# Prompt attention with the values two steps behind the scores, opened together with them, and six probability buffers

## The chip, the cores and the metric

The kernel runs on one core of a Trainium2 chip. The core has a matmul engine (PE, with its weight loads shown as PEld), three engines for elementwise work (DVE, ACT, POOL) and SP, whose queue issues most of the DMA transfers. Each engine works through its own instructions in the order in which they were written down when the kernel was built; an instruction that has to wait for a semaphore holds up all that stand behind it on that engine. The metric is the time of one execution on the device in microseconds (us); lower is better.

## The reference

One layer of a decoder for a prompt of 1024 tokens and a batch of 8 x 4 new tokens, in float32. What matters here is the attention of the prompt: 8 heads of 64 in 2 groups of 4 heads that share keys and values, with three branches that are added with a gate each.

```python
def nsa_block(q, gates, q_pos, ctx, kw, vw, w_pos):
    ...
    p_c = masked_softmax(s_c, m_c)                      # compressed blocks of keys
    o_c = jnp.einsum('bqghc,bcgd->bqghd', p_c.astype(vc.dtype), vc)
    ...
    p_s = masked_softmax(s_s, m_s)                      # chosen blocks (for the prompt: all that are valid)
    o_s = jnp.einsum('bqghn,bgqnd->bqghd', p_s.astype(v_sel.dtype), v_sel)
    ...
    p_w = masked_softmax(s_w, m_w)                      # the last 512 keys and the query itself
    o_w = jnp.einsum('bqghw,bwgd->bqghd', p_w.astype(vw.dtype), vw)
    g = jax.nn.sigmoid(gates.astype(jnp.float32)).astype(q.dtype)
    return g[..., 0:1] * o_c + g[..., 1:2] * o_s + g[..., 2:3] * o_w
```

The prompt has 16 blocks of 64 keys and 16 are chosen, so the second branch sees every key up to the query. Before and after the attention stand a combined input projection, a convolution module, gates and two output projections, for prompt and new tokens alike.

## The kernel before

The kernel has four stages. The input projection and the attention of the new tokens (with gathers from the paged caches) fill the first 850 us. The prompt attention follows, woven with the last tiles of the input projection, the norm and the pointwise product of the convolution and the merge of the second branch. At about 1265 us the output products begin (tiles `v`).

The order on each engine is not written by hand. The code yields pieces of several streams in turn (`_mixed`, `late_weave`: so many pieces of the prompt stream for so many of the others), and a scheduler with a timing model of its own then places the instructions on the engines by that order and by when it thinks that inputs and buffers are ready. A change in the prompt stream therefore re-plans all engines from its first step on.

The prompt stream (`prompt_stream`, L1523) runs over the 2 groups `g`, the 8 query tiles `qt` of 128 queries and two pairs of heads `hp`: 32 steps. A step has these parts:

- `queries` (L1295) loads the queries of a tile twice, one below the other, into `ldq`. ACT copies the upper half to `Qst` (rounded for the fast matmul format) and the lower half to `ldh`, and DVE puts the rest of the rounding into the lower half of `Qst`.
- `prompt_scores` (L1413) makes for both heads `e` and both branches `i` (0: all keys, 1: the window) scores in a bank pair `S` (two of them), subtracts the maximum (DVE, L1470), takes the exponential with its sum (ACT, L1426) into a buffer `P`, and scales P by gate over sum: on DVE for branch 0 (L1485), for branch 1 on POOL for one head (L1487) and on ACT for the other (L1489). `P0` and `P1` have four buffers each, two of which one step takes.
- `prompt_values` (L1492) transposes the probabilities in groups of four 128 x 128 blocks into a bank `tr` (PE, L1512; three banks, shared with the woven streams), splits a group into a rounded half `pth` (ACT, L1334) and the rest `ptl` (DVE, L1335), three buffers each, and multiplies both with the values into `acc` (PE, L1502 and L1503), one group behind the transposes.
- `prompt_open` (L1402) does the same for the compressed branch: it transposes `Pc`, splits it, and its two products (L1409, L1410) are the first to write `acc`. There is one bank `acc` (`ps_a`). `put` (L1338) reads it out at the end of a tile: two copies on ACT (L1342, L1343) and two additions on DVE (L1346).
- `prompt_c` (L1367) makes the compressed probabilities `Pc` for both groups while `g` is 0 and stores them in `pc_d`, from where group 1 loads them; `Pc` has two buffers.

Scores of step n are woven with the values of step n-1 (L1536 to L1540). `prompt_open` of a tile is called when its first step's scores are done (L1542).

Woven with this are `branches` (L1549: three loads `obt`, `obl` of the new tokens' branches, two additions on DVE, four small transposes on PE, L1559; the loads use buffers of `pth` and `ptl`), `points` (L1685: loads `x` from `s_d`, ACT's rounding `sh`, POOL's rest `sl`, products with `pwh`, `pwl`), and `late` (L1733: the merge, then `gated` tiles with loads `gat`, and four loads `wa` of w_pa that ACT copies at L1748).

Of the kernel before, what the change touches and what calls it, by code (L numbers as in the profile page):

```python
# [119 lines left out]
def _emit(ctx, tc, I, O, dbg=None, stop=None):  # L120
# [1150 lines left out]
    with ExitStack() as P3:  # L1271
# [23 lines left out]
        def queries(g, qt):  # L1295
            Qst = pq.tile([128, 4, 128], F32R, name="Qst", tag="Qst", bufs=2)
            x = pq.tile([128, 4, 128], F32, name="ldq", tag="ldq", bufs=2)
            src = qT_d[g * 256:(g + 1) * 256, qt * 128:(qt + 1) * 128].rearrange("(h d) q -> d h q", h=4)
            sp.dma_start(x[:64], src)
            sp.dma_start(x[64:], src)  # L1300
            hi = pq.tile([128, 4, 128], F32R, name="ldh", tag="ldh", bufs=1)
            for o, r, on in ((Qst, slice(0, 64), QC & 1), (hi, slice(64, 128), QC >> 1)):
                if on:
                    pool.tensor_copy(o[r], x[r])
                else:
                    act.activation(o[r], x[r], AF.Copy)
            dve.tensor_tensor(Qst[64:], x[64:], hi.bitcast(F32)[64:], op=ALU.subtract)
            return Qst
# [93 lines left out]
        def prompt_open(g, qt, Pc):  # L1402
# [10 lines left out]
        def prompt_scores(g, qt, hp, Qst, S):  # L1413
# [10 lines left out]
            def exps(e, i, sv, W, n):  # L1424
                P = pP.tile([128, 1024 if i == 0 else 640], F32, name="P", tag=f"P{i}", bufs=4)
                act.activation(P[:, :W].rearrange("p (c w) -> p c w", c=n), sv, AF.Exp,  # L1426
                               bias=nm[:, e, i:i + 1], accum_out=l[:, e, i:i + 1])
                Ps.append(P)
# [63 lines left out]
        def prompt_values(g, qt, hp):  # L1492
            Ps, Vs, lo_k = PU.pop((g, qt, hp))
            acc = PU[g, qt]
# [28 lines left out]
        def prompt_stream():  # L1523
            prev = None
            Q = queries(0, 0)
            for g in range(2):
                S = stacks(g)
                for qt in range(8):
# [3 lines left out]
                    else:  # L1532
                        P = pq.tile([128, 8, 64], F32, name="Pc", tag="Pc", bufs=2)
                        sp.dma_start(P.rearrange("p a c -> p (a c)"), pc_d[qt * 128:(qt + 1) * 128, :])
                    for hp in range(2):
                        streams = [(prompt_scores(g, qt, hp, Q, S), 2 if qt < 4 else 4)]  # L1536
                        if prev:
                            n = min(prev[1], 4) + prev[1] + 2
                            streams.append((prompt_values(*prev), (n + 1) // 2))
                        yield from _mixed(*streams)  # L1540
                        if hp == 0:
                            prompt_open(g, qt, P)  # L1542
                        elif (g, qt) != (1, 7):
                            Q = queries(*divmod(g * 8 + qt + 1, 8))
                        prev = (g, qt, hp)
            yield from prompt_values(*prev)
# [330 lines left out]
```

## Time and profile before

| what | value |
|---|---|
| three runs, median (lowest to highest) | 1423.98 us (1417.65 to 1424.43) |
| the profiled execution | 1420.95 us |
| its span, first to last instruction | 1419.2 us |
| mean granted clock of PE in it | 0.979 of 2.4 GHz |
| prompt attention in the span | about 848 to 1265 us |
| busy share of PE, DVE, ACT, POOL over the span | 94%, 76%, 51%, 46% |

PE is busy nearly all the time, but a matmul's end is modelled, so busy does not mean at its peak; what can be read well is where PE stands idle and who ended it. A granted clock of 1.00 is 2.4 GHz, 0.50 is 1.2 GHz, and values between them are means over a stretch.

### The profile page before, as it was taken

The page shows a single profiled execution, that of the slowest core. Times are in us where ns is not written, and L with a number is a line of the kernel's source. Part 1 is how long each engine was busy: PE and PEld are TensorE (multiplying, and loading weights), DVE is VectorE, ACT ScalarE, POOL GpSimd, SP SyncE. Part 2 cuts the span into 40 slices and gives each one's busy share as a digit, 9 for nine tenths or more (in the row PEclk, how much of TensorE's full clock was granted, in tenths as well). Part 3 has the DMA queues.
Part 4 walks back from the last instruction along what each step waited for, and adds up shares of the span by engine and source line. Part 5 has one row for each costly group of instructions (what it writes and reads, how often), then busy time and mean ns, then how long its engine had stood idle before and what let it go on. Part 6 is the DMA issues. An engine that isn't in the chain of part 4 may idle for free.

```text
span 1419.2 us, 25556 instructions
## 1 busy us (share of the span) xinstructions
PE 1337.1 (94%) x9689; PEld 1202.6 (85%) x9689; DVE 1078.7 (76%) x1915; ACT 720.5 (51%) x1323; POOL 646.0 (46%) x537
## 2 busy tenths in 40 slices
PE   5999989879999999999999999999889999899997
PEld 4998989879899999788877898889778899789876
DVE  7888886878887848887956945978777988888233
ACT  5454445545443634554554335766666876653311
POOL 2388884886884605554454202434564221321200
PEclk9999999989999999999999999999979999999999
DMA  7666566566665418797788565543553633416421
GB/s 256 189 193 215 179 183 209 188 212 197 196 203 195 153 52 298 236 356 265 262 301 287 173 165 163 154 121 98 177 152 98 192 118 102 133 51 196 182 92 46
DMA packets 184358, 256.87 MB, mean 181 GB/s; under 512 B 27348, under 2 KB 137508, under 8 KB 183971
## 3 DMA queue, kind: packets, MB, share of 16 engines
q1 hardware_dynamic: 137114, 121.42, 28.3%
q0 software_dynamic: 36608, 125.85, 26.6%
q10 hardware_dynamic: 10512, 7.96, 1.8%
q8 instruction: 76, 1.25, 0.3%
q14 instruction: 48, 0.39, 0.1%
HBM read 215.56 MB, written 44.20 MB: 183 GB/s over the span
## 4 chain that ended last, share of the span: by engine, by line
PE 66%; DVE 11%; DMA 9%; issue 6%; POOL 4%; ACT 3%; SPq 1%; DVEq 0%; POOLq 0%; ACTq 0%
PE mm L193 7%; PE mm L192 7%; PE mm L194 7%; PE x L521 7%; POOL G L573 4%; PE v L192 3%; PE v L194 3%; PE v L193 3%; PE tr L192 3%; PE tr L194 3%; DMA G<-in_cache_k_cmp,idxc 3%; PE tr L193 3%; PE tr L1512 3%; DMA G<-in_cache_v_cmp,idxc 2%; PE x L1032 2%
## 5 line engine op out<-in xcount | busy, mean ns | idle before, releaser
L192 PE MATMUL mm<-xh,wh 128*128 128x352 f32 x840 | 276.4, 329 | 2.8 <-ACT xh L401 2.0
L193 PE MATMUL mm<-xl,wh 128*128 128x352 f32 x840 | 275.1, 327 | 0.9 <-DVE xl L407 0.9
L194 PE MATMUL mm<-xh,wl 128*128 128x352 f32 x840 | 274.7, 327 | 0.0
L573 POOL DMA_INDIRECT G<-in_cache_v_cmp,idxc x128 | 167.0, 1304 | 79.6 <-DVE T L531 29.1
L573 POOL DMA_INDIRECT G<-in_cache_k_cmp,idxc x128 | 163.8, 1280 | 86.4 <-DMA w2bk<-in_w_k 30.0
L531 DVE STREAM_TRANSPOSE T<-G 128x512 f32<-128x512 f32 x260 | 167.9, 686 | 38.1 <-DMA G<-in_cache_v_cmp,idxc 17.9
L535 ACT ACTIVATE Th<-T 128x2048 fp32r<-128x2048 f32 x66 | 124.7, 1889 | 94.6 <-DVE T L531 41.0
L193 PEld LDWEIGHTS mm<-xl,wh 128*128 128x128 f32 x840 | 159.0, 189 | 10.1 <-issue 8.3
L192 PEld LDWEIGHTS mm<-xh,wh 128*128 128x128 f32 x840 | 158.5, 189 | 9.3 <-issue 6.2
L194 PEld LDWEIGHTS mm<-xh,wl 128*128 128x128 f32 x840 | 158.7, 189 | 5.4 <-issue 4.9
L539 DVE TENSOR_TENSOR Tl<-T,Th 128x2048 fp32r<-128x2048 f32 x66 | 147.4, 2237 | 15.9 <-issue 9.5
L1227 DVE SCALAR_TENSOR_TENSOR acc<-ub,dwT,acc 128x1024 f32<-128x1024 f32 x120 | 153.6, 1280 | 1.0
L1335 DVE TENSOR_TENSOR ptl<-tr,pth 128x512 fp32r<-128x512 f32 (+1 forms) x152 | 100.2, 669 | 20.9 <-ACT pth L1334 20.0
L1426 ACT ACTIVATE P<-S,sc 128x640 f32<-128x640 f32 (+7 forms) x128 | 89.2, 701 | 35.9 <-PE tr L1512 18.3
L1334 ACT ACTIVATE pth<-tr 128x512 fp32r<-128x512 f32 (+1 forms) x152 | 87.6, 585 | 35.6 <-PE tr L1512 27.9
L1487 POOL TENSOR_SCALAR P<-P,sc 128x640 f32<-128x640 f32 (+4 forms) x32 | 53.1, 1659 | 108.4 <-DVE sc L1480 66.2
L1019 POOL DMA_INDIRECT KG<-in_cache_k_slc,idxs x56 | 63.5, 1133 | 71.6 <-ACT kg L1046 53.8
L1019 POOL DMA_INDIRECT VG<-in_cache_v_slc,idxs x56 | 67.4, 1203 | 56.5 <-PE y L1104 37.3
L521 PE MATMUL x<-Tl,w1hv 128*128 128x256 f32 (+1 forms) x264 | 77.6, 294 | 6.7 <-DVE Tl L539 6.7
L1503 PE MATMUL acc<-ptl,vs 128*128 128x256 f32 x264 | 73.1, 299 | 10.2 <-DVE ptl L1335 10.1
L521 PE MATMUL x<-Tl,w1hk 128*128 128x256 f32 (+1 forms) x264 | 77.9, 295 | 5.1 <-DVE Tl L539 5.1
L1512 PE MATMUL tr<-ident,P 128*128 128x128 f32 x528 | 80.7, 278 | 1.7 <-ACT var L1613 0.6
(469 smaller groups left out, 3588.2 us busy)
## 6 DMA issues: line engine op xcount, KB each, us to landing
wt<-in_w_in SPq DMA_DIRECT2D x42, 512.0 KB
m_d<-stg SPq DMA_DIRECT2D x16, 528.0 KB
x<-in_x_prompt SPq DMA_DIRECT2D x16, 512.0 KB
mb<-m_d SPq DMA_DIRECT2D x24, 176.0 KB
t_d<-mb SPq DMA_DIRECT2D x24, 176.0 KB
mb<-t_d SPq DMA_DIRECT2D x24, 176.0 KB
ma<-m_d SPq DMA_DIRECT2D x24, 176.0 KB
ldq<-qT_d SPq DMA_DIRECT2D x32, 128.0 KB
```

The costliest lines, as they stand in the source:

```text
L192: pe.matmul(ps, wh, xh, start=i == 0, stop=False)
L193: pe.matmul(ps, wh, xl, start=False, stop=False)
L194: LAST_MM[0] = pe.matmul(ps, wl, xh, start=False, stop=i == n - 1)
L521: pe.matmul(o, w[:, s], t[:, :, :, s // 2, s % 2], start=s == 0 and i == 0, stop=s == 7 and i == 2)
L531: dve.transpose(T[:, gi], G)
L535: act.activation(Th[:, :m], T[:, :m], AF.Copy)
L539: eng.tensor_tensor(Tl[:, r], T[:, r], Th.bitcast(F32)[:, r], op=ALU.subtract)
L573: pool.indirect_dma_start(out=G, out_offset=None, in_=tab, in_offset=bass.IndirectOffsetOnAxis(ap=idxc[:, b * 16 + gi:b * 16 + gi + 1], ax ...
L1019: pool.indirect_dma_start(out=dst, out_offset=None, in_=pools[n], in_offset=bass.IndirectOffsetOnAxis(ap=col, axis=0))
L1227: eng.scalar_tensor_tensor(a, x, dwT[:, ct, j:j + 1], a, op0=ALU.mult, op1=ALU.add)
L1335: dve.tensor_tensor(lo[:, :w], t[:, :w], hi.bitcast(F32)[:, :w], op=ALU.subtract)
L1512: pe.transpose(t[:, (2 * x + e) * 128:(2 * x + e + 1) * 128], Ps[e * 2 + i][:, c0:c0 + 128], ident)
```

## The change

Four edits. The queries are rounded by one activation over all 128 partitions, and DVE subtracts in place; the buffer `ldh` is gone. `P0` and `P1` have six buffers each. The stream keeps a list `prev` of up to two steps, so that the values that are woven with the scores of step n are those of step n-2, and two steps of values follow the last scores. `prompt_open` is called at the start of a tile's first `prompt_values`, and takes `Pc` from `PU`.

```diff
--- before.py
+++ after.py
@@ -1298,13 +1298,8 @@
             src = qT_d[g * 256:(g + 1) * 256, qt * 128:(qt + 1) * 128].rearrange("(h d) q -> d h q", h=4)
             sp.dma_start(x[:64], src)
             sp.dma_start(x[64:], src)
-            hi = pq.tile([128, 4, 128], F32R, name="ldh", tag="ldh", bufs=1)
-            for o, r, on in ((Qst, slice(0, 64), QC & 1), (hi, slice(64, 128), QC >> 1)):
-                if on:
-                    pool.tensor_copy(o[r], x[r])
-                else:
-                    act.activation(o[r], x[r], AF.Copy)
-            dve.tensor_tensor(Qst[64:], x[64:], hi.bitcast(F32)[64:], op=ALU.subtract)
+            act.activation(Qst, x, AF.Copy)
+            dve.tensor_tensor(Qst[64:], x[64:], Qst.bitcast(F32)[64:], op=ALU.subtract)
             return Qst
 
         def stacks(g):
@@ -1399,7 +1394,8 @@
 
         PU, SW = {}, shift_windows()
 
-        def prompt_open(g, qt, Pc):
+        def prompt_open(g, qt):
+            Pc = PU.pop((g, qt))
             acc = ps_a.tile([128, 512], F32, name="acc", tag="acc")
             t = bank(ps_t, "tr")
             for h in range(4):
@@ -1422,7 +1418,7 @@
             nm, l, rr = sc[:, 0], sc[:, 1], sc[:, 2]
 
             def exps(e, i, sv, W, n):
-                P = pP.tile([128, 1024 if i == 0 else 640], F32, name="P", tag=f"P{i}", bufs=4)
+                P = pP.tile([128, 1024 if i == 0 else 640], F32, name="P", tag=f"P{i}", bufs=6)
                 act.activation(P[:, :W].rearrange("p (c w) -> p c w", c=n), sv, AF.Exp,
                                bias=nm[:, e, i:i + 1], accum_out=l[:, e, i:i + 1])
                 Ps.append(P)
@@ -1491,6 +1487,8 @@
 
         def prompt_values(g, qt, hp):
             Ps, Vs, lo_k = PU.pop((g, qt, hp))
+            if hp == 0:
+                prompt_open(g, qt)
             acc = PU[g, qt]
             todo = [(1, k) for k in range(lo_k[1], qt + 1)] + [(0, k) for k in range(qt + 1)]
             ao = acc[:, hp * 256:(hp + 1) * 256]
@@ -1521,7 +1519,7 @@
                 put(acc, g, qt)
 
         def prompt_stream():
-            prev = None
+            prev = []
             Q = queries(0, 0)
             for g in range(2):
                 S = stacks(g)
@@ -1532,18 +1530,19 @@
                     else:
                         P = pq.tile([128, 8, 64], F32, name="Pc", tag="Pc", bufs=2)
                         sp.dma_start(P.rearrange("p a c -> p (a c)"), pc_d[qt * 128:(qt + 1) * 128, :])
+                    PU[g, qt] = P
                     for hp in range(2):
                         streams = [(prompt_scores(g, qt, hp, Q, S), 2 if qt < 4 else 4)]
-                        if prev:
-                            n = min(prev[1], 4) + prev[1] + 2
-                            streams.append((prompt_values(*prev), (n + 1) // 2))
+                        if len(prev) == 2:
+                            old = prev.pop(0)
+                            n = min(old[1], 4) + old[1] + 2
+                            streams.append((prompt_values(*old), (n + 1) // 2))
                         yield from _mixed(*streams)
-                        if hp == 0:
-                            prompt_open(g, qt, P)
-                        elif (g, qt) != (1, 7):
+                        if hp and (g, qt) != (1, 7):
                             Q = queries(*divmod(g * 8 + qt + 1, 8))
-                        prev = (g, qt, hp)
-            yield from prompt_values(*prev)
+                        prev.append((g, qt, hp))
+            for old in prev:
+                yield from prompt_values(*old)
             yield
 
         def branches():
```

Three places of the built order. Lines of the new file are 5 lower from L1308 to about L1400, 4 lower to L1490 and 2 to 1 lower behind it, so ACT's L1329 is the L1334 of before, L1422 is L1426, L1747 is L1748, and so on.

ACT, near the end of the stream, from the third copy of w_pa (`ch<-wa`) to the fourth. `pth` is a transposed half, `P,sc<-S,sc` an exponential with its sum, `tm` the read-out of `acc`. Before:

```order
L1364 ACTIVATE oah<-gat 128x2x128
L1342 ACTIVATE tm<-acc 64x256
L1343 ACTIVATE tm<-acc 64x256
L1426 ACTIVATE P,sc<-S,sc 128x640
L1748 ACTIVATE ch<-wa 128x4x256 x2
L1334 ACTIVATE pth<-tr 128x512
L1364 ACTIVATE oah<-gat 128x2x128
L1334 ACTIVATE pth<-tr 128x512
```

After:

```order
L1747 ACTIVATE ch<-wa 128x4x256
L1422 ACTIVATE P,sc<-S,sc 128x1024
L1329 ACTIVATE pth<-tr 128x256
L1359 ACTIVATE oah<-gat 128x2x128
L1329 ACTIVATE pth<-tr 128x512 x2
L1422 ACTIVATE P,sc<-S,sc 128x1024
L1337 ACTIVATE tm<-acc 64x256
L1338 ACTIVATE tm<-acc 64x256
L1747 ACTIVATE ch<-wa 128x4x256
L1329 ACTIVATE pth<-tr 128x512
```

Before, the third and the fourth copy follow each other; now eight instructions stand between them.

PE, at the last tile (group 1, tile 7), from the last product of the tile before (`acc<-ptl,vs`, of a pair that starts with `acc<-pth,vs`) to the products of the opening (`acc<-pth,vcs_559`, `acc<-ptl,vcs_559`). Before:

```order
L1503 MATMUL acc<-ptl,vs 128x256
L1512 MATMUL tr<-ident,P 128x128 x4
L1459 MATMUL S<-kh,Qst 128x320
L1461 LDWEIGHTS identb
L1461 MATMUL S<-medge,identb 128x128
L1464 MATMUL S<-kl,Qst 128x320
L1459 MATMUL S<-kh,Qst 128x320
L1463 LDWEIGHTS identb
L1463 MATMUL S<-mdiag,identb 128x128
L1464 MATMUL S<-kl,Qst 128x320
L1512 MATMUL tr<-ident,P 128x128 x8
L1409 MATMUL acc<-pth,vcs_559 128x512
```

After:

```order
L1500 MATMUL acc<-pth,vs 128x256
L1501 MATMUL acc<-ptl,vs 128x256
L1510 MATMUL tr<-ident,P 128x128 x12
L1405 MATMUL acc<-pth,vcs_559 128x512
L1406 MATMUL acc<-ptl,vcs_559 128x512
```

The same product and the same opening; the score instructions of the last step that stood between them have moved ahead of this place, and twelve transposes are left.

SP, from the loads of the convolution's weights `pwr` to the third load of the branches (`obl<-ob_d_76`) and on. Before:

```order
L1676 DMA pwr<-in_pw_w 128x4x128
L1553 DMA obl<-ob_d_75 32x2x256
L1676 DMA pwr<-in_pw_w 128x4x128
L1691 DMA x<-s_d 128x4x352
L1700 DMA gbt<-gb_d 128x352
L1553 DMA obl<-ob_d_76 32x2x256
L1700 DMA gbt<-gb_d 128x352
L1691 DMA x<-s_d 128x4x352
```

After:

```order
L1180 DMA out<-in_cache_v_win 16x2x4064
L1552 DMA obl<-ob_d_75 32x2x256
L1675 DMA pwr<-in_pw_w 128x4x128 x2
L1690 DMA x<-s_d 128x4x352
L1699 DMA gbt<-gb_d 128x352 x2
L1690 DMA x<-s_d 128x4x352
L1663 DMA w<-in_w_pb 128x4x128
L1641 DMA s_d<-ct 128x4x176
L1345 DMA oT_d<-tm 128x2x128
L1663 DMA w<-in_w_pb 128x4x128
L1552 DMA obl<-ob_d_76 32x2x256
L1641 DMA s_d<-ct 128x4x176
```

Before, the third load was issued between the first loads `x` and `gbt`; now it stands behind both loads of `x`, a store `s_d<-ct`, the store `oT_d<-tm` of a finished tile and two loads of w_pb.

## Rows read from the trace of the kernel before

**Rows 1.** The page, part 1: busy us, share of the span, instructions.

```profile
PE 1337.1 (94%) x9689; PEld 1202.6 (85%) x9689; DVE 1078.7 (76%) x1915; ACT 720.5 (51%) x1323; POOL 646.0 (46%) x537
```

**Rows 2.** Windows of 10 us: length, busy PE, PEld, DVE, ACT, POOL, clock, DMA.

```profile
1025.00:1035.00 10.00, 2.97 (x9) 1.72 (x10) 8.97 (x10) 4.09 (x7) 9.81 (x9) 0.68 1.08 294
...
1035.00:1045.00 10.00, 8.40 (x34) 7.24 (x35) 7.03 (x10) 6.17 (x10) 8.16 (x6) 0.50 0.54 137
...
1155.00:1165.00 10.00, 10.00 (x74) 9.40 (x73) 7.75 (x15) 8.33 (x19) 1.28 (x1) 1.00 0.38 109
...
1225.00:1235.00 10.00, 6.01 (x29) 5.06 (x30) 8.88 (x13) 5.68 (x11) 4.60 (x2) 0.66 0.55 162
...
sum 440.00, PE 408.38 PEld 374.21 DVE 354.94 ACT 286.85 POOL 164.22; mean PE 9.28 PEld 8.50 DVE 8.07 ACT 6.52 POOL 3.73
```

**Rows 3.** Waits of PE, 848 to 1265 us: total us, times, longest.

```profile
PE acc L1503 <- DVE ptl L1335: 10.1, 11, 2.6
...
PE S L1459 <- ACT P L1426: 7.2, 3, 6.1
...
PE tr L192 <- DVE ptl L1335: 3.1, 1, 3.1
...
PE acc L1502 <- ACT pth L1334: 2.7, 1, 2.7
...
PE tr L1406 <- POOL Pc L1394: 0.5, 1, 0.5
...
PE tr L1512 <- POOL P L1487: 0.3, 1, 0.3
...
PE tr L1512 <- DVE P L1485: 0.3, 1, 0.3
```

**Rows 4.** Chain that ended last, at 1024, 1032 and 1219: start, us, what.

```profile
1023.94 7.52 DMA obl<-ob_d
...
1032.24 3.08 DVE z L1386
...
1219.46 5.30 DMA wa<-in_w_pa
```

**Rows 5.** Timelines of ACT, POOL, PE near 1030: start, us, instruction, idle before.

```profile
1030.44 1.38 ACT L1692 ACTIVATE sh<-x 128x1408 fp32r<-128x1408 f32 x1 [3.61 <-DMA x<-s_d]
...
1031.90 3.39 POOL L1693 TENSOR_TENSOR sl<-x,sh 128x1408 fp32r<-128x1408 f32 x1 [0.19 <-ACT sh L1692]
...
1025.92 0.39 PE L1503 MATMUL acc<-ptl,vs 128*128 128x256 f32 x1 [2.37 <-DVE ptl L1335]
...
1032.65 0.79 PE L1459 MATMUL S<-kh,Qst 128*128 128x512 f32 x1 [6.11 <-ACT P L1426]
```

**Rows 6.** Timelines of ACT and PE near 1226.

```profile
1224.79 1.06 ACT L1748 ACTIVATE ch<-wa 128x1024 fp32r<-128x1024 f32 x1 [3.82 <-DMA wa<-in_w_pa]
...
1226.38 0.42 PE L1502 MATMUL acc<-pth,vs 128*128 128x256 f32 x1 [2.69 <-ACT pth L1334]
...
1229.41 0.58 PE L1503 MATMUL acc<-ptl,vs 128*128 128x256 f32 x1 [2.61 <-DVE ptl L1335]
```

**Rows 7.** Timelines of PE, ACT and DVE near 1247: the turn of the accumulator bank.

```profile
1220.44 1.03 PE L1512 MATMUL tr<-ident,P 128*128 128x128 f32 x8
...
1246.80 0.28 PE L1503 MATMUL acc<-ptl,vs 128*128 128x256 f32 x1
...
1247.12 0.38 ACT L1342 ACTIVATE tm<-acc 64x256 f32<-64x256 f32 x1 [0.41 <-PE acc L1503]
...
1248.66 0.85 DVE L1346 TENSOR_TENSOR tm<-acc,tm 64x256 f32<-64x256 f32 x2
...
1249.65 0.47 PE L1409 MATMUL acc<-pth,vcs 128*128 128x512 f32 x1 [0.21 <-ACT P L1426]
```

**Rows 8.** Durations: by line (ns min/median/max), then groups (busy us, mean ns).

```profile
L1306 ACT ACTIVATE ldh<-ldq x16: 627/628/632, 835.2 to 1163.7; 64x512 fp32r<-64x512 f32 x16
...
L1386 DVE TENSOR_SCALAR z<-z x8: 156/167/3139, 873.1 to 1032.2; 128x8 f32<-128x8 f32 x8
...
L1334 ACT ACTIVATE pth<-tr 128x512 fp32r<-128x512 f32 x144 | 84.7, 597 | 35.5 <-PE tr L1512 27.9 <-PE acc L1409 5.1 <-PE tr L1406 1.7
...
L1426 ACT ACTIVATE P<-S,sc 128x1024 f32<-128x1024 f32 x8 | 8.9, 1116 | 6.0 <-PE tr L1512 6.0
```

## The prediction

> **What bounds the kernel now.** I read the shares first: the matmul engine is busy 94% of the span [rows 1], so time can only be won where it stands still or runs at the lower clock. The change touches the prompt attention alone, which runs from about 848 to 1265 us, so the second view is that stretch in pieces of 10 us [rows 2]. The reader is to see that the idle time is not spread: of 440 us (845 to 1285) PE is busy 408.38, which leaves 31.6 us idle, and whole stretches such as 1155 to 1165 have none, while 1025 to 1035 has 7.0 us of it. The granted clock is 1.00 (the 2.4 GHz level) but for the pieces behind the long gaps: 0.68 and 0.50 around 1035, 0.66 around 1230, which means all or part of them at the 1.2 GHz level.
>
> The third view says for whom PE waited [rows 3]. Products of the values wait for the low half of transposed probabilities (10.1 and, with a projection caught behind it, 3.1 us) and for the high half (2.7 us); scores wait for a score bank that the exponentials must free (7.2 us). What the change's delay of the values is made for, transposes that wait until probabilities are scaled, is the smallest entry: 0.3 us for POOL's scaling and 0.3 us for DVE's. The opening of a tile waits 0.5 us for its compressed probabilities.
>
> The fourth view is the chain and the engines' own rows at the two dear places. At 1024 to 1033 DVE stood behind the third load of the sample branches (7.52 us from issue to landing) and ACT behind a load of the convolution's rows (3.61 us idle); ACT's next exponential was what the scores needed, and PE lost 6.11 us in one piece [rows 4, 5]. At 1220 to 1229 ACT stood 3.82 us behind the last load of w_pa, with the transposed halves queued behind it, and PE lost 2.69 and 2.61 us [rows 4, 6]. Both are loads that an in-order queue met too early. They have nothing to do with how old the probabilities are.
>
> **The change, part by part.** The sum is made against the profiled execution, 1420.95 us (span 1419.2, 1.75 around it). The median of the three runs is 1423.98, 3.0 higher, and that is added at the end.
>
> *No work on PE.* The built order holds the same PE instructions in another order; DVE's and POOL's kinds and counts stay too. So busy time at full clock is unchanged, and everything below is waiting.
>
> *Values two steps behind, six buffers.* The transposes' 0.6 us go, since the scaling ends a step before they come, and so do the 0.5 us of the opening's wait for the compressed probabilities: 1.1 us off, at worst 0 if other work is late at these spots. The buffers themselves cost nothing: a score step may run as far ahead of the values as before (four buffers for a lag of one, six for a lag of two, two of each kind taken by each step).
>
> *Queries with one activation.* Sixteen ACT instructions of 0.628 us [rows 8] go, 10.0 us of ACT. I put that at 0: PE's waits for ACT's exponentials are 7.2 us, of which 6.11 stood behind the load [rows 3, 5], so at most 1.1 us can come from it. The subtraction on DVE stays and waits for one activation as before; the queries are loaded a step ahead, which covers it, and without that cover the 0.628 us saved would shorten the wait.
>
> *The copies of w_pa.* The scheduler re-plans everything behind the first step, and here that matters: in the old order the third and the fourth copy stand in one row on ACT; in the new one eight instructions stand between them, two exponentials of 1.1 us and two transposed halves of 0.6 us [rows 8] among them, 3.4 us without the small ones. ACT met the load 3.82 us too early [rows 6], so nearly all of that wait is covered. PE's loss there is 2.69 + 2.61 us, plus the half clock behind it: a mean of 0.66 over 10 us is 6.8 us at the 1.2 GHz level, of which PE stood idle some 3, and the other 4 held work that takes 2 at full clock. The whole is 7.3. DVE also had to wait for loads of gates in this stretch, which stay, so I take 3 off, with 7.3 and 0 as the ends.
>
> *The sample branches' loads.* In the new order their third load stands behind the store of a finished tile, a store that DVE must release, instead of ahead of it; and the copy of the cache window and two loads of x are issued before it. So it is issued only after the tile's last product, two copies on ACT and two additions on DVE. Behind it wait DVE's second addition, the four small transposes on PE, and then twelve transposes and all products. From the additions' end PE still has the opening and four products, about 1 us; the load takes 7.5 us as it did [rows 4], or about 5.3 as the w_pa load did on a quieter queue, and the addition 0.7. PE would wait 5 to 8 us here, against 6.11 + 2.37 us [rows 5] now. On the other side, the small DVE operation on z that took 3.08 us of the chain [rows 4] now stands ahead of the wait. Net I take 2 off; the ends are 14 off (no gap at all, 8.5 us; and of the 16.4 us at the 1.2 GHz level from 1025 to 1045, some 11 held work, of which half comes back) and 5 more (the two waits in a row instead of side by side).
>
> That operation's row bears on a rule: it took 3.139 us where its median is 0.167 [rows 8], while POOL ran a subtraction of 3.39 us that started 0.3 us earlier [rows 5]. The Trainium skill (page "SBUF — State Buffer", section "Who interferes with whom") says that DVE in its two-port mode and GpSimd share a port pair, and that whichever comes second is blocked for the whole instruction. The trace agrees with its 3.08 us. By the rule POOL's scalings, which also move, would cost as much wherever they meet such an operation; the sum does not use it.
>
> *The opening with the values.* There is one accumulator bank. Between a tile's last product and the next tile's opening ACT copies twice and DVE adds twice. In the last tile that took 2.57 us: the product ends at 1247.08, the additions run from 1248.66 for 0.85, the opening starts at 1249.65 after an idle 0.21 us [rows 7]. In the old order eight score instructions and twelve transposes cover this; in the new one only twelve transposes do, which at 8 in 1.03 us [rows 7] are under 1.5 us, 1.3 by their spacing. So about 1.3 us of waiting is new here. Counting the rows between last product and opening in the same way for all 15 openings, one more (tile 7 of the first group) has 1.2 us of cover, two have 2.1 and 2.4, the other eleven 2.9 or more; in the old order one has 2.1 and the others 2.8 or more. The shortfall to 2.57 is 3.2 us against 0.4. I add 2.5. The ends are 0 (the copies come quicker when ACT is less busy) and 9 (below).
>
> *The rest.* The small gaps from 875 to 965 are re-mixed: 0, within 3 either way.
>
> Sum: -1.1 - 3 - 2 + 2.5 = -3.6 us, 1417.4 for the profiled execution, and with the 3.0 of the median **1420 us**.
>
> **The rivals.**
>
> *Most of the waiting goes (faster).* If values that are two steps old let PE run past every late half, the waits for both halves (10.1 + 3.1 + 2.7 = 15.9 us) go and with them some 3 us of the half clock: 1423.98 - 19 = 1405. For it: these are the largest entries. Against it: a half is late because ACT or DVE, in order, stand behind a load or each other; the transposes still feed the same three buffers, and their age does not shorten that. The Trainium skill (page "Perfetto Trace Analysis", section "Optimization Strategy") says that the same gap repeating on the engine that should be saturated can mean too few buffers; by it six buffers would give this case. Here the gaps are not alike (6.11, 2.69, 2.61, 2.37 us), and the middle of the stage has none.
>
> *The one accumulator bank becomes the wait (slower).* If ACT and DVE are late, so that the turn from last product to opening takes 4.3 instead of 2.57 us, ten openings of the new order fall short, by 15.2 us in all, against 6.1 us in the old: 9 more, 1433. It decides from about 4 us on. For it: DVE is busy 8.97 of 10 us around 1030 and 8.88 around 1230 [rows 2]. Against it: in the one turn shown ACT began 0.04 us after the product.
>
> *The loads in a row (slower).* ACT's wait for x and DVE's wait for the third load no longer lie side by side: the upper end of that term, 5 us, and 3 us more of half clock behind it, 1423.98 + 8 = 1432.
>
> *It does not do what it says.* The scheduler may pull the values as close to the scores as they were; then only a re-mix is left, 1424.
>
> **How the numbers follow.** The forecast, with its own spread of about 7 us either way, gets 0.55; most waiting gone 0.20; the accumulator bank 0.15; loads in a row 0.05; no real change 0.05. About 0.5% (7.1 us, so 1416.9 and 1431.1) is what a measurement of this kernel can tell from no change. Faster: the first rival's 0.20 and 0.10 of the forecast's lower side, 0.30. Slower: 0.13 of the bank, 0.05 of the loads, 0.18. The same: 0.52. The range takes in half of the first rival and half of the slower ones: 1405 to 1434.
>
> **What would show it.** In the new profile the transposes' waits for scaled probabilities are gone; the copy of w_pa has little idle time before it, and the gap around 1226 is under 2 us; a gap of 5 us or more stands before the four small transposes of the branches; the openings show a wait for DVE's additions of about 1 us at the last tile. Wrong would be: PE idle in this stage under 15 us (the first rival), or openings with several us each (the second). A gap in the middle of the stage, where there is none now, would be something that this sum does not hold.

## The result: 0.83% slower, and the profile after

The changed kernel takes 1431.01 us (median of ten, 1425.26 to 1436.07) against 1418.42 us for the kernel before in the same sitting (ten, 1414.58 to 1424.43): ratio of the means 1.0083, interval 1.0057 to 1.0108. In a second sitting (run e17, below) it is 1.0101 (1.0043 to 1.0159). So it is slower by 12.6 and 16.5 us in the medians; the forecast was 1420 us, 3.6 less than the time then taken for the kernel before. The profiled execution is 1436.07 us, the longest of its ten, with a span of 1434.3, 15.1 longer than that of before.

The page of the changed kernel, first part (busy us, share of the span, instructions), answers to [rows 1]:

```profile
PE 1342.8 (94%) x9689; PEld 1204.9 (84%) x9689; DVE 1084.0 (76%) x1915; ACT 710.6 (50%) x1307; POOL 655.7 (46%) x537
```

PE's count is the same, its busy time 5.7 us more; ACT's is 9.9 us less, which is the queries' work that went. Windows of 10 us of the changed kernel (columns as in [rows 2]):

```profile
965.00:975.00 10.00, 8.45 (x38) 7.60 (x37) 7.10 (x20) 2.71 (x6) 4.10 (x4) 0.68 0.23 65
...
1025.00:1035.00 10.00, 5.90 (x27) 3.89 (x26) 7.60 (x14) 6.77 (x15) 8.11 (x12) 0.76 1.07 342
...
1035.00:1045.00 10.00, 1.52 (x6) 1.09 (x4) 6.25 (x7) 4.80 (x6) 9.84 (x7) 0.50 1.12 341
...
1045.00:1055.00 10.00, 9.61 (x54) 8.90 (x55) 4.52 (x8) 4.37 (x9) 7.63 (x6) 0.72 0.30 86
...
1075.00:1085.00 10.00, 6.39 (x25) 6.04 (x26) 5.54 (x13) 5.14 (x16) 1.63 (x2) 0.66 0.47 132
...
1155.00:1165.00 10.00, 10.00 (x74) 9.34 (x73) 8.31 (x16) 5.98 (x13) 3.46 (x2) 1.00 0.41 123
...
sum 440.00, PE 401.74 PEld 365.65 DVE 348.07 ACT 271.90 POOL 160.07; mean PE 9.13 PEld 8.31 DVE 7.91 ACT 6.18 POOL 3.64
```

The pieces that stand out are no longer two. The transition at 1025 to 1055 is still there and longer, and 965 to 975 and 1075 to 1085 lie at a mean of 0.68 and 0.66 of the clock. In the kernel before they ran at full speed:

```profile
965.00:975.00 10.00, 9.40 (x70) 9.03 (x71) 7.30 (x22) 5.67 (x13) 4.01 (x4) 1.00 0.46 144
...
1075.00:1085.00 10.00, 10.00 (x75) 9.67 (x74) 6.54 (x15) 6.28 (x19) 3.31 (x4) 1.00 0.41 109
```

Stretches such as 1155 to 1165 have no idle time, as before. PE's waits from 848 to 1285 us (total us, times, longest) answer to [rows 3]:

```profile
PE acc L1501 <- DVE ptl L1330: 10.3, 9, 2.2
...
PE tr L1558 <- DVE obt L1555: 8.9, 1, 8.9
...
PE S L1455 <- ACT P L1422: 5.0, 6, 2.1
...
PE tr L1510 <- DVE ptl L1330: 3.8, 1, 3.8
...
PE S L1455 <- DVE Pc L1374: 1.6, 1, 1.6
...
PE acc L1405 <- DVE tm L1341: 1.5, 2, 1.0
...
PE tr L1402 <- POOL Pc L1389: 0.2, 1, 0.2
```

Transposes that wait for a scaling are gone, as forecast, and the opening waits 0.2 us for its probabilities instead of 0.5. New are the branches' transposes with 8.9 us in one piece and scores that wait behind small things on ACT and DVE. By stretches, between rows that both kernels have (the first score, the branches' four transposes, the first output product, the last):

| stretch | before, us | after, us |
|---|---|---|
| first score to the branches' transposes | 165.6 | 177.9 |
| from there to the first output product | 228.1 | 230.0 |
| output products | 148.7 | 151.4 |

The same work lies in each to within seven instructions of PE. Most of the loss is in the first stretch. The rows of PE at its places, and of those that PE waited for (start, us, instruction, idle before it and who ended it):

```profile
920.48 0.41 PE L1455 MATMUL S<-kh,Qst 128*128 128x320 f32 x1 [1.60 <-DVE Pc L1374]
...
967.72 0.45 PE L1455 MATMUL S<-kh,Qst 128*128 128x384 f32 x1 [1.02 <-ACT P L1422]
...
1028.19 0.50 PE L1455 MATMUL S<-kh,Qst 128*128 128x512 f32 x1 [1.04 <-ACT P L1422]
...
1031.58 0.63 PE L1455 MATMUL S<-kh,Qst 128*128 128x320 f32 x1 [2.07 <-ACT P L1422]
...
1034.47 0.77 PE L1405 MATMUL acc<-pth,vcs 128*128 128x512 f32 x1 [0.98 <-DVE tm L1341]
...
1045.39 0.63 PE L1558 MATMUL tr<-ident,obt 32*128 32x32 f32 x4 [8.86 <-DVE obt L1555]
...
1043.59 1.74 DVE L1555 TENSOR_TENSOR obt<-obt,obl 32x512 f32<-32x512 f32 x1 [3.72 <-DMA obl<-ob_d]
```

The first two stops, 1.60 and 1.02 us, are small, but work of 3.4 and 6.7 us at the 1.2 GHz level follows them. The last is the one that the prediction described: DVE stands behind the third load of the branches, then adds, and PE waits 8.86 us before the four transposes. Some 1.1 us of that is not the load: the addition took 1.74 us beside POOL's subtractions, and the one before it, of the same shape, 0.65.

For all runs below, one number does without the first 760 us, which differ by some us from execution to execution: the time from PE's 5601st matmul (up to there the order is alike in all) to the last. It is 646.1 us before and 663.5 after. Of that, PE's idle time (gaps over 0.15 us) is 30.8 and 40.4 us, and the work done at the 1.2 GHz level 19.1 and 32.2 us (from windows of 0.5 us between 860 and 1310), half of which is lost (products of 256 columns follow each other by 0.12 us at 1074 us and by 0.22 at 1036). That explains 9.6 + 6.5 = 16.1 of the 17.4 us: no work was added, PE stands still more often and runs slow behind it.

### The profile page after: what moved, and what is told of

Same layout as the page of the kernel before. It is cut to its first block, busy times and chain, and to the rows that moved or that the text cites. A ratio compares the mean times of both kernels' runs of the same rounds, so it can differ in the third digit from the quotient of the medians.

```text
span 1434.3 us, 25553 instructions
## 1 busy us (share of the span) xinstructions
PE 1342.8 (94%) x9689; PEld 1204.9 (84%) x9689; DVE 1084.0 (76%) x1915; ACT 710.6 (50%) x1307; POOL 655.7 (46%) x537
## 5 line engine op out<-in xcount | busy, mean ns | idle before, releaser
L573 POOL DMA_INDIRECT G<-in_cache_k_cmp,idxc x128 | 169.7, 1326 | 80.0 <-DMA w2bk<-in_w_k 29.1
L573 POOL DMA_INDIRECT G<-in_cache_v_cmp,idxc x128 | 170.0, 1328 | 78.1 <-DVE T L531 31.3
L1422 ACT ACTIVATE P<-S,sc 128x640 f32<-128x640 f32 (+7 forms) x128 | 89.3, 704 | 37.9 <-DVE sc L1466 14.6
L1329 ACT ACTIVATE pth<-tr 128x512 fp32r<-128x512 f32 (+1 forms) x152 | 87.0, 587 | 40.3 <-PE tr L1510 34.8
L1501 PE MATMUL acc<-ptl,vs 128*128 128x256 f32 x264 | 73.7, 301 | 10.8 <-DVE ptl L1330 10.3
```

The lines of the kernel that those rows point to most:

```text
L573: pool.indirect_dma_start(out=G, out_offset=None, in_=tab, in_offset=bass.IndirectOffsetOnAxis(ap=idxc[:, b * 16 + gi:b * 16 + gi + 1], ax ...
```

## The experiments

**Theories.** *Lag*: values that run two steps behind hold score banks or buffers longer, and PE waits for scores. *Opening*: the rival of the prediction, one accumulator bank. *Any re-planning*: the order before is a favourable one among many; whatever changes the plan loses some us in new small stops, whether the change is good or not. From e5 on a fourth is named, *buffers*: six buffers let the plan put scores further ahead, and that costs in any order.

**e1, the queries alone.**

```diff
-            hi = pq.tile([128, 4, 128], F32R, name="ldh", tag="ldh", bufs=1)
-            for o, r, on in ((Qst, slice(0, 64), QC & 1), (hi, slice(64, 128), QC >> 1)):
...
+            act.activation(Qst, x, AF.Copy)
+            dve.tensor_tensor(Qst[64:], x[64:], Qst.bitcast(F32)[64:], op=ALU.subtract)
```

> The kernel before with one of the four edits alone: the queries rounded by one activation over 128 partitions (ldh gone). Theory 'lag' (the two-step delay itself makes the 12.6 us, through score banks that come free too late): this stays at the time before, ratio 0.997 to 1.003. Theory 'opening' (the moved opening and its one accumulator bank): the same, 0.997 to 1.003. Theory 'any re-planning' (every change of the stream shuffles the instructions near 867 to 1045 us, and the order before was a lucky one): 3 to 10 us more, ratio 1.003 to 1.007 or above, with other gaps in that stretch.

Measured: 1418.64 us, ratio 1.0025 (1.0001 to 1.0049). Ten microseconds less of ACT's work gain nothing. This too is another order (some 460 of PE's instructions stand elsewhere, from 880 us on), and it costs less than 'any re-planning' expected, 1.003 or more.

**e2, the opening alone.** `prompt_open(g, qt)` at the start of the values with `hp == 0`, all else as before.

> The kernel before with the opening moved into the first values of a tile, and nothing else: lag of one step, four probability buffers, two activations for the queries. Theory 'lag': ratio 0.997 to 1.003. Theory 'opening': the loss of after is here, ratio 1.006 to 1.010, with openings that wait for the accumulator bank. Theory 'any re-planning': between 1.000 and 1.010, in gaps that are neither.

Measured: 1417.88 us, ratio 1.0009 (0.9982 to 1.0036). The built program has every instruction of every engine at the same place as before: with a lag of one the scheduler puts the opening where it was. So this run is a second measurement of the kernel before, and shows the noise: 644.6 against 646.1 us for the part from the 5601st matmul on.

**e3, the lag taken back; e4, the buffers taken back.** From the changed kernel:

```diff
-                        if len(prev) == 2:
+                        if len(prev) == 1:
```

```diff
-                P = pP.tile([128, 1024 if i == 0 else 640], F32, name="P", tag=f"P{i}", bufs=6)
+                P = pP.tile([128, 1024 if i == 0 else 640], F32, name="P", tag=f"P{i}", bufs=4)
```

> The changed kernel with the lag set back to one step; the single activation for the queries, six buffers and the moved opening stay. Theory 'lag': back to the time before, ratio 0.997 to 1.003, and PE idle between the first scores and the branches' transposes falls from 21.9 to about 15 us. Theory 'opening': no gain against after, ratio 1.006 to 1.010. Theory 'any re-planning': anything from 1.000 to 1.010.

> The changed kernel with four probability buffers of each kind instead of six, so that the scores cannot run further ahead of the values than before. Theory 'lag': the delay stays, so the loss stays or grows, ratio 1.008 to 1.015, since a score step must now also wait for buffers that are held one step longer. If instead the loss comes from scores that run too far ahead of the values, four buffers take part of it back: ratio 1.000 to 1.006. Theory 'any re-planning': unlike after by 3 us or more either way.

Measured: e3 1428.34 us, ratio 1.0077 (1.0043 to 1.0110); e4 1445.97 us, 1.0193 (1.0140 to 1.0246). e3 leaves out the main step of the change and is as slow: the lag is not needed for a loss of this size. Its stops are others, mostly of products for late halves. Nor does the wait that *lag* named stand out in the changed kernel: before scores PE waits 10.2 us in all there, and 9.2 in the kernel before (848 to 1285 us). e4 is the slowest of all, with 11.7 us before the branches' transposes and 4.3 us at an opening. The waits of ACT (848 to 1290 us), first in the changed kernel, then in e4, show exponentials that wait longer for transposes to free a buffer:

```profile
ACT P L1422 <- PE tr L1510: 13.4, 10, 4.9
```

```profile
ACT P L1422 <- PE tr L1510: 23.9, 15, 3.3
```

That fits a lag of two with too few buffers; but the kernel before has 18.3 us of the same wait, so whether the buffers or the new order make e4's 1.1% over the changed kernel is not settled. What e3 leaves open is why six buffers at a lag of one should cost anything, unless it is the new order as such; no run has the six buffers alone.

**e5 to e8, e11 to e14: other orders of both kernels.** One planning number is changed, by how many pieces of the prompt the weave takes for the others; instructions, buffers and lag stay. The orders part inside the prompt attention, not earlier.

```diff
-PN = 230
+PN = 222
```

and 226, 234, 238, on the kernel before and on the changed one.

> The kernel before with one planning number changed (PN 222 instead of 230: the weave takes 3% fewer pieces of the prompt per piece of the other streams); the instructions are the same, their order is not from 1200 us before the end on PE's side. Theory 'any re-planning' (the order before is a favourable one among many): ratio 1.002 to 1.010. Theory 'buffers' (six buffers let the plan put scores further ahead, and that costs in any order): 0.997 to 1.003.

> The kernel before with PN 234 instead of 230, the other direction. Theory 'any re-planning': ratio 1.002 to 1.010. Theory 'buffers': 0.997 to 1.003.

> The changed kernel with PN 222 instead of 230. Theory 'any re-planning': a scatter about the same middle as re-planned orders of before, ratio to before 1.000 to 1.010, unlike after by several us. Theory 'buffers': 1.006 to 1.011, as after.

> The changed kernel with PN 234 instead of 230. Theory 'any re-planning': ratio 1.000 to 1.010, unlike after by several us. Theory 'buffers': 1.006 to 1.011, as after.

> The kernel before with PN 226 instead of 230. If the order before is a favourable one among many ('any re-planning'): ratio 1.003 to 1.012 like PN 222 and 234 (1.0114, 1.0074). If it is a smooth optimum around 230: 1.000 to 1.005.

> The changed kernel with PN 226 instead of 230. 'Any re-planning': ratio to before between 1.003 and 1.010, like PN 222, 230 and 234 of the changed kernel (1.0057, 1.0083, 1.0055). If the two-step delay itself costs something in every order, the changed kernel's middle lies above that of before at other PN; if it gains something, below: by the numbers so far below, by 2 to 8 us.

> The kernel before with PN 238 instead of 230. 'Any re-planning': ratio 1.003 to 1.012. A smooth optimum around 230: above the 1.0074 of PN 234, 1.010 or more.

> The changed kernel with PN 238 instead of 230. 'Any re-planning': ratio 1.003 to 1.010, no better or worse than before with PN 238 by more than 5 us.

Measured, as ratios to the kernel before (in the same sitting) with the interval, and the time from the 5601st matmul on in each run's one profile:

| PN | kernel before | changed kernel | before, us | changed, us |
|---|---|---|---|---|
| 222 | 1.0114 (1.0066 to 1.0161) | 1.0057 (1.0026 to 1.0088) | 653.8 | 649.4 |
| 226 | 1.0019 (0.9985 to 1.0053) | 1.0025 (0.9982 to 1.0069) | 650.6 | 649.4 |
| 230 | 1 | 1.0083 (1.0057 to 1.0108) | 646.1 | 663.5 |
| 234 | 1.0074 (1.0047 to 1.0102) | 1.0055 (1.0030 to 1.0079) | 656.4 | 651.4 |
| 238 | 1.0050 (1.0019 to 1.0081) | 1.0053 (1.0016 to 1.0090) | 656.2 | 653.5 |

The mean of the five ratios is 1.0051 on the left and 1.0055 on the right, that of the five times 652.6 and 653.4 us. Over orders the change moves nothing that can be told; against the one order that was there it loses. Five orders of each tell this no closer than to about half a percent (an estimate from the scatter of the ratios), so the 3.6 us that were forecast are neither borne out nor excluded; without PN 230 the means are 1.0064 and 1.0048, on the forecast's side. *Buffers* does not hold in any order: it expected at most 1.003 in e5 and e6 and at least 1.006 in e7 and e8, and all four came out otherwise. A smooth optimum around 230 is not borne out either: it would have put PN 238 on the left at 1.010 or more (e13). In e5 the branches' transposes cost more than in the changed kernel:

```profile
1041.92 0.63 PE L1559 MATMUL tr<-ident,obt 32*128 32x32 f32 x4 [13.55 <-DVE obt L1556]
```

**e9, e10, e15, e16: the branches ahead of the prompt.** The wait that the prediction named is taken out by calling the branches before the first 40% of the prompt instead of behind it; in e9 PE's order ahead of that point stays nearly the same, in e10 less so.

```diff
+        branches()
         late_weave(SPLIT, (GT, 3 * SUB * (24 - NG) - HEAD), (norms(), 5 * NC + 1, 1))
-        branches()
```

> The kernel before with the call of the branches (three loads, two additions, four small transposes) moved from behind the first 40% of the prompt to ahead of it; PE's order is the same up to 1015 us but for those four transposes. Theory 'load' (the stop at 1026 to 1033 us is the third load's 7.5 us, and it goes when the load is out of that place): PE's idle there falls from 8.5 to under 4 us and the half clock behind it shrinks, 6 to 12 us less, ratio 0.992 to 0.996. Theory 'place' (the loads of the convolution, weights and x, hold the stage back there anyway): idle of 6 us or more stays at 1020 to 1040, ratio 0.997 to 1.003. Theory 'any re-planning' adds up to 10 us behind 1040: ratio 1.000 to 1.006.

> The changed kernel with the same move of the branches. Theory 'load': the 8.9 us that PE stands before the four small transposes go, and half of the 9 us of work at half clock behind it: 8 to 13 us less than after, ratio to before 0.998 to 1.003. Theory 'place': 3 us less at most, ratio 1.005 to 1.010, with a wait for x or for weights in its place.

> The kernel before with PN 222 and with the branches' call moved ahead of the first 40% of the prompt. With PN 222 alone PE stands 13.55 us before the branches' four small transposes, and the ratio is 1.0114. Theory 'branches' (most of what a new order costs is this one wait, which the order before has placed well): the wait goes, some of it comes back as waits for halves and scores as in the early version of before, ratio 1.000 to 1.006. Theory 'spread' (the cost of a new order is spread over many small stops): 1.008 to 1.012.

> The changed kernel with PN 226 and the branches' call moved ahead. PN 226 alone gives 1.0025. Theory 'branches': 0.994 to 1.001, about the time before or better. Theory 'spread': 1.001 to 1.007, another order with another set of small stops.

Measured: e9 (on the kernel before) 1414.41 us, ratio 0.9971 (0.9948 to 0.9993), a version that beats both; the ratio lies in the range of 'place', the idle time (below) between the two theories. e10 (on the changed one) 1429.79, 1.0084 (1.0055 to 1.0113). e15 (before, PN 222) 1430.93, 1.0082 (1.0044 to 1.0119), where PN 222 alone has 1.0114. e16 (changed, PN 226) 1425.98, 1.0024 (0.9991 to 1.0057), where PN 226 alone has 1.0025. By the ratios 'place' holds in e10, and 'spread' in e15 and e16. PE in e9 at the transition, where [rows 5] had 2.37 and 6.11 us, and in e10 the stop there with the instruction of DVE and of POOL that led to it:

```profile
1028.59 0.38 PE L1503 MATMUL acc<-ptl,vs 128*128 128x256 f32 x1 [1.67 <-DVE ptl L1335]
...
1031.43 0.50 PE L1459 MATMUL S<-kh,Qst 128*128 128x512 f32 x1 [1.66 <-ACT P L1426]
...
1034.50 0.42 PE L1459 MATMUL S<-kh,Qst 128*128 128x320 f32 x1 [0.62 <-ACT P L1426]
...
1038.60 0.57 PE L1459 MATMUL S<-kh,Qst 128*128 128x512 f32 x1 [1.96 <-ACT P L1426]
```

```profile
1045.54 0.58 PE L1501 MATMUL acc<-ptl,vs 128*128 128x256 f32 x1 [5.11 <-DVE ptl L1330]
...
1038.91 2.45 DVE L1476 SCALAR_TENSOR_TENSOR sc<-sc,gp 128x4 f32<-128x4 f32 x1
...
1038.14 3.19 POOL L1692 TENSOR_TENSOR sl<-x,sh 128x1408 fp32r<-128x1408 f32 x1
```

The loads gone, e9 stops four times for 5.9 us instead of 8.5 (10.1 with two small stops behind those). In e10 the 8.86 us are gone and 5.11 us stand in their place: a DVE instruction that takes 0.15 us elsewhere took 2.45 beside POOL's 3.19, which is 2.3 us of it. One wait out of an order gives back little by the medians, since the next is close behind; in e15, where the wait was 13.55 us, no more than 0.3% came back, inside both intervals. For e10 the profile says more: its part from the 5601st matmul on is 654.9 us against 663.5, and whether some of that came back is not settled, since the intervals of the ratios leave room for some 5 us.

**e17, the changed kernel again.**

> The changed kernel itself, for a second profile (the first one, 1436.07 us, is the longest of its ten executions). Expected: ratio 1.006 to 1.011, and the same stops at the same places: 8 to 9 us before the branches' transposes, 3 to 4 us at the keys of the second group, about 6 us in the last 45 us of the prompt; if the sum of the stops is smaller by some 5 us, the first profile overstates the loss by as much.

Measured: 1436.72 us, ratio 1.0101 (1.0043 to 1.0159), profile of 1439.42 us. The stops are the same to a few hundredths (1.60, 1.02, 2.06, 1.01, 8.86 us), and the part from the 5601st matmul on is 663.6 us against 663.5. The loss belongs to the order, not to the execution; its size in the profiles may be some us too large, since this profile, like the first, is of the longest execution of its run.

**e18, shorter instructions on POOL.** e9 with POOL's two longest kinds cut into four:

```diff
-                    pool.tensor_tensor(sl, x, sh.bitcast(F32), op=ALU.subtract)
+                    for k in range(4):
+                        pool.tensor_tensor(sl[:, k], x[:, k], sh.bitcast(F32)[:, k], op=ALU.subtract)
...
-                pool.tensor_tensor(cl[:, :, es], wa, ch.bitcast(F32)[:, :, es], op=ALU.subtract)
+                for k in range(4):
+                    pool.tensor_tensor(cl[:, k, es], wa[:, k], ch.bitcast(F32)[:, k, es], op=ALU.subtract)
```

> The early version of the kernel before (run e9: ratio 0.9971), in which POOL makes the rest of the convolution's rows (3.2 us each, three times) and of w_pa (2.38 us each, four times) in four pieces instead of one; the order on the other engines stays nearly the same. In every profile all DVE instructions that take longer than usual lie beside a POOL instruction, up to 2.98 us longer, and the stops of PE at 1038 and at 1221 to 1224 us stand behind such ones. Theory 'port' (DVE waits until POOL's instruction has ended): with pieces of 0.6 to 0.9 us no DVE instruction beside them takes more than 1 us longer, these stops of 1.96, 2.07 and 2.65 us shrink by half or more, ratio 0.992 to 0.996. Theory 'it waits anyway' (DVE waits for each piece again, or the loads end last): the stops stay within 0.7 us, ratio 0.996 to 1.000.

Measured: 1414.99 us, ratio 0.9966 (0.9938 to 0.9995), no better than e9 and in the range of 'it waits anyway'. Near the copies of w_pa it did what was hoped (DVE's scaling, first e9, then e18):

```profile
1220.97 2.55 DVE L1485 TENSOR_SCALAR P<-P,sc 128x896 f32<-128x896 f32 x1
```

```profile
1231.15 1.10 DVE L1485 TENSOR_SCALAR P<-P,sc 128x896 f32<-128x896 f32 x1
```

and PE's two stops behind it fell from 2.07 and 2.65 to 0.61 and 1.22 us (a stop of 1.83 us stands ahead of them, of 0.93 in e9). At the transition it did no good, and PE stands still as long as in e9 (7.0 and 7.1 us): POOL issued the pieces and two more subtractions back to back, and DVE's small operation waited through several of them.

```profile
1043.27 4.26 DVE L1386 TENSOR_SCALAR z<-z 128x8 f32<-128x8 f32 x1
...
1044.99 2.52 POOL L1682 TENSOR_TENSOR pwl<-pwr,pwh 128x512 fp32r<-128x512 f32 x2
```

So 'port' held at one place and 'it waits anyway' at the other.

## Why the prediction was wrong

The measured time lay inside the range, and the direction was wrong: faster by 3.6 us was forecast, slower by 12.6 us is measured. The table has what PE lost in each stretch, as idle time plus half of the work at 1.2 GHz, in two profiles of the old order (the kernel before, e2) and two of the new one (the changed kernel, e17); the boundaries lie where PE has no stop, and their times are those of the kernel before.

| stretch | old order, us | new order, us | difference of the means |
|---|---|---|---|
| first score to 1015 us | 6.4, 7.3 | 14.0, 14.8 | +7.5 |
| 1015 to 1060, the branches' loads | 15.8, 11.4 | 17.5, 16.6 | +3.5 |
| 1060 to 1100, the second group's keys | 5.1, 6.4 | 7.6, 7.4 | +1.8 |
| from there to the copies of w_pa | 0, 0 | 1.0, 1.0 | +1.0 |
| copies of w_pa to the first output product | 10.3, 10.6 | 9.9, 10.9 | 0.0 |
| output products | 1.7, 1.7 | 4.8, 6.3 | +3.9 |

The prediction had terms for the second and the fifth row. The other four, which it held at 0, are 14 of some 18 us. Step by step:

- *The base.* The three runs' median stood 3.0 us above the profiled execution; ten runs have 1418.42, 2.5 below it. Adding 3.0 was reading noise.
- *No work on PE.* Right. For each of the kernels run, the time from the 5601st matmul on, less PE's idle time and half of its work at 1.2 GHz, is 603 to 612 us, 606 in the kernel before and 607 in the changed one.
- *Two steps behind, six buffers: -1.1.* Right in kind: the transposes' waits are gone. They were worth this little, and e3 loses as much without the lag.
- *Queries: 0.* Right in kind: e1 gains nothing from ten us less on ACT (1.0025).
- *The copies of w_pa: -3.* The wait for the load is gone from ACT, as read from the order. The gain is not: the last 469 instructions of PE before the first output product take 76.3 us before and 76.0 after. In the place of 2.69 + 2.61 us [rows 6] there are stops of 1.53 and 2.23 us for halves that DVE made late beside POOL:

```profile
1224.87 0.39 PE L1501 MATMUL acc<-ptl,vs 128*128 128x256 f32 x1 [1.53 <-DVE ptl L1330]
...
1234.37 0.39 PE L1501 MATMUL acc<-ptl,vs 128*128 128x256 f32 x1 [2.23 <-DVE ptl L1330]
...
1221.66 2.55 DVE L1357 TENSOR_TENSOR gat<-gat,oT 128x256 f32<-128x256 f32 x1 [0.89 <-DMA gat<-ga_d]
...
1231.87 1.85 DVE L1360 TENSOR_TENSOR oal<-gat,oah 128x256 fp32r<-128x256 f32 x1
...
1221.56 2.38 POOL L1748 TENSOR_TENSOR cl<-wa,ch 128x1024 fp32r<-128x1024 f32 x1 [10.48 <-ACT ch L1747]
...
1230.69 2.74 POOL L1748 TENSOR_TENSOR cl<-wa,ch 128x1024 fp32r<-128x1024 f32 x1
```

Alone these two DVE instructions take 0.41 us. The reading of [rows 6] was wrong in the same point. The prediction put both stops down to ACT's wait for the load, but the second, 2.61 us, stood behind a scaling on DVE that took 2.52 us beside POOL and 0.67 three microseconds later; the order on ACT could not take it away:

```profile
1226.23 2.52 DVE L1485 TENSOR_SCALAR P<-P,sc 128x896 f32<-128x896 f32 x1
...
1229.28 0.67 DVE L1485 TENSOR_SCALAR P<-P,sc 128x896 f32<-128x896 f32 x1
...
1225.92 2.35 POOL L1749 TENSOR_TENSOR cl<-wa,ch 128x1024 fp32r<-128x1024 f32 x1 [2.49 <-ACT ch L1748]
```

The section of the Trainium skill that the prediction named (page "SBUF — State Buffer", section "Who interferes with whom") was thus not a side remark: beside the two-port mode it says that a DVE instruction with two inputs in SBUF contends with a GpSimd (POOL) instruction that reads SBUF. The trace agrees with it at both new stops (2.55 and 1.85 us beside POOL's 2.38 and 2.74), and the sum left it out.
- *The branches' loads: -2, ends -14 and +5.* Read right from the order: 5 to 8 us before the four transposes were forecast, 8.86 came. What was not seen is that the two stops before it (1.04 and 2.07 us) and the opening (0.98) would stand in front of it instead of inside it. The rival of the loads in a row, which gave 1432 and so the number nearest to the 1431.0 measured, came true in this part: the stops do stand in a row. That its number fits is luck, since the stretch lost 3.5 us more than before in the mean, where this rival had 8 more and the term itself 2 less, and most of the loss lies elsewhere.
- *The opening: +2.5.* Mechanism right, size 1.5 us: 0.98 at 1034 and 0.47 at the last tile, where 1.3 was forecast. By the rows, twelve transposes are a little over 1.5 us, not under. The rival of the accumulator bank, which gave 1433, did not happen: no opening of the changed kernel waited several us.
- *Most of the waiting goes* (1405) did not happen either: products and transposes behind late halves wait 14.1 us (10.3 + 3.8) after, and 15.9 were counted before.
- *The rest: 0, within 3 either way.* This is the step that failed, by 14 us. From the first score to 1015 us PE idles 8.9 us against 6.4 and does 10.1 us of work at 1.2 GHz against none; the loads of the second group's keys cost 3.8 us and 6.1 us of slow work, before 3.1 and 3.4; the output products take 2.7 us longer, behind two DVE instructions of 0.52 us that took 5.02 us together beside POOL. Before, the output products had 1.7 us of idle time and no slow work, with 2.88 us for the same two instructions. The keys and the output products are not among what the change edits. The row of PE at the output products, and DVE's, after and then before:

```profile
1295.98 0.43 PE L192 MATMUL v<-oah,ch 128*128 128x352 f32 x1 [3.06 <-DVE ma L1796]
...
1290.47 5.02 DVE L1783 SCALAR_TENSOR_TENSOR hl<-ma,hh 128x352 fp32r<-128x352 f32 x2 [1.95 <-ACT hh L1782]
...
1278.12 2.88 DVE L1784 SCALAR_TENSOR_TENSOR hl<-ma,hh 128x352 fp32r<-128x352 f32 x2 [2.02 <-ACT hh L1783]
```

Instead of zero, a new order of this kernel costs on average: the four orders that PN gives beside the old one lie 0.2 to 1.1% above it on the kernel before, 0.6% or 9 us in the mean. The old order has the best of the five outcomes (1 lies within the interval of 226). The prediction's last rival, in which only a re-mix is left, came nearest in kind and priced it at 0; its condition, values pulled back to the scores, is not what the trace shows, since the transposes' waits are gone.

What stays open: what makes one order better than another is not one wait. The runs show only that it is the sum of a dozen or more stops of 0.8 us and above and of the slow clock behind them, and that taking one out moves the medians little.

## What to carry to other kernels

When a scheduler re-plans a kernel from an edit on, the edit is measured together with a new order. Price that first: change a neutral planning number up and down, on the kernel before and on the changed one, and compare the two sets; here the spread over orders (0 to 1.1%) was larger than the difference that the edit made between the means (0.03%, known to about half a percent). And a zero for "the rest" needs such a comparison behind it: an order at hand that is better than its neighbours can only lose by being planned anew.

## What the runs showed of the hardware

DVE's instructions have fixed times here but for POOL. From 860 to 1310 us, in all kernels run, no DVE instruction that ran without a POOL instruction beside it took more than 0.03 us over the usual time of its shape (the median, over all runs, of those without POOL beside them). All longer ones lie beside POOL, 33.4 us in sum before and 38.1 after (those over 0.25 us), and only on instructions that read and write SBUF alone: the 152 `ptl`, which read a transposed bank, are never longer, though 58 and 53 of them ran beside POOL. The sum does not follow the time over the runs: it is 29.6 us in e2, which has the order of the kernel before, 36.0 in e17, and 32.8 in e4, the slowest. That it counts where they fall is a reading, not shown by a run of its own. An instruction of 0.16 us was held 4.26 us through four POOL instructions that followed each other (e18).

The clock does not answer the same stop in the same way each time: behind the 1.43 and 0.75 us at 873 to 875 us of the changed kernel there is no slow work in the first profile, and 3.4 us of it in the second. At the transition the 1.2 GHz level held for 17.1 us in the kernel before and for 10.2 in e2, which has the same order.
